# Operand addresses, the order of the first forms and products, and later background work in an fp32 decoder trunk on one core

## The chip, the cores and the metric

The kernel runs on one core of one Trainium2 chip. The metric is the device time of one execution in microseconds, smaller is better; the kernel before takes 1950.9 us (median of three runs, 1949.98 to 1951.61). TensorE (PE) multiplies, VectorE (DVE) and ScalarE (ACT) work on tiles in SBUF and PSUM, GpSimd (POOL) and SyncE (SP) here mainly issue DMAs.

## The reference

A decoder trunk of two layers on x of 512 tokens by 1024 features, all in float32. Each layer is a half-step feed-forward part, a mixer, and another half-step feed-forward part:

```
x = x + 0.5 * swiglu(rmsnorm(x, ffn1_norm[i]), ffn1_gate[i], ffn1_up[i], ffn1_down[i])
h = rmsnorm(x, mix_norm[i])
x = x + (diff_fox_mixer(h, ...) if i % 2 == 0 else s5_mixer(h, ...))
x = x + 0.5 * swiglu(rmsnorm(x, ffn2_norm[i]), ffn2_gate[i], ffn2_up[i], ffn2_down[i])

swiglu(h, w_gate, w_up, w_down) = (silu(h @ w_gate) * (h @ w_up)) @ w_down     # 1024 -> 2816 -> 1024
rmsnorm(x, g) = x * rsqrt(mean(x * x) + 1e-6) * g
```

The mixer of layer 0 is attention (two kinds of heads in parallel), that of layer 1 a complex diagonal state-space layer (S5) with a gated output.

## The kernel before

**Stages.** Six stages run one after the other: the first feed-forward part, attention, the second and third feed-forward parts, the S5 stage, the fourth feed-forward part. x stays in SBUF, transposed: eight tiles `x[:, d]` of 128 features by 512 tokens. Weights stream from HBM.

**Products.** A float32 product is three fp32r matmuls: high part of the weights by high part of the tokens, high by low, low by high (`prod`, L476, in the feed-forward parts; `mm3`, L211 to L213, elsewhere). The weight block is the operand that is loaded into TensorE, the token operand streams, 256 columns at a time in L476 and 512 in the down product and elsewhere. ScalarE casts the high part `wh` of a weight block (L118), VectorE takes the low part `wl` (L121, L123). Eight `raw` buffers of 512 KB receive the blocks: SyncE issues the loads (L75), GpSimd a second load that is added to the first where a sum of two blocks is wanted (L85).

**The feed-forward product.** Gate and up weights are taken in pairs j of blocks, and a pair's products are a Strassen-like set of seven, P1 to P7. They multiply sums of weight blocks by seven "forms" of the tokens, kept as high and low parts in `Fh[:, s]` and `Fl[:, s]` for slots s = 0 to 6. Slots 0 to 2 are x scaled (`form_plain`), slots 3 to 6 are sums of these (`form_sum`, L297), split in two by a cast on ScalarE (L305) and a subtraction on VectorE (L306). `SLOT` says which product uses which slot: P1 0, P2 1, P3 2, P5 3, P6 4, P7 5, P4 6. `ffn_plan()` is the order of the steps: "first" (P1, P2 and P5 of pair 0 together), P6 0, P1 1, P3 0, then for each pair j from 1 on P5 j, P7 j-1, P2 j, P6 j, P4 j-1, P1 j+1, P3 j, and from pair 3 on two steps of the down product (`down`, tiles `ps_d`) in between. The last step writes what is left of the down product by tiles d = 0 to 7 (`last`).

**Forms and statistics.** Before the first part, `forms_start` writes all forms, and the sums of squares follow: eight squares on ScalarE, seven additions into `acc` on VectorE (`norm_sum`). In the later parts the forms of the next stage are written tile by tile as x is finished (`forms`, `form_tile`). `stats1` sums `acc` over features by four matmuls against a column of ones (L373) and takes the reciprocal root on VectorE; `stats2` turns and spreads it to the tile `R`. Both stand behind early steps of each part.

**Background work.** `k.bg` holds generators that are not needed at once: `attn_setup` and `s5_tables` in the first part, `s5_rotate` and `s5_ops` in the second and third. After each step `tick(k, rate)` lets them issue `rate` pieces of work, up to a piece that says "wait"; rates are 0.9 in the first part, 0.8 in the second and third, and the steps of the down product use 0.8 of the rate. `drain(k)` issues all that is left; it stands behind the first part and, as the `leave` of the third, inside `last()` ahead of the loop over d. `s5_ops` goes round by units: matmuls of `e`, tables `t`, `y` and a sum `kq` on VectorE, stores of them to DRAM on GpSimd's queue (`dW`, `dY`, `dK`, L194), eight loads `tr` of what was stored in `dK` (L202), 16 copies `to` of them on ScalarE (L1524), and stores `dT`.

**Addresses.** Tiles of one pool stand one behind the other in a partition of SBUF. The token tiles (`Fh`, `Fl`, `xh`, `xl`, `F`) stand at 32 modulo 512 bytes, the weight tiles and the gate's `ah` and `al` at 288; the difference is 256. A small tile `oss` of 24 floats, of which 16 are used, stands ahead of the token tiles.

Instructions of one engine run in the order in which the program issues them; that order is set by the code above, and a wait holds all that stands behind it on its engine.

## Time and profile before

| | |
|---|---|
| median of three runs | 1950.9 us (1949.98 to 1951.61) |
| profiled execution, time | 1949.56 us |
| profiled execution, span | 1947.8 us |
| TensorE busy | 1851.9 us, 95% |
| VectorE busy | 1412.5 us, 73% |
| ScalarE busy | 870.6 us, 45% |
| GpSimd busy | 246.5 us, 13% |
| matmuls of the feed-forward product, 128x256 | 7392 |
| HBM | 171 GB/s over the span |

The span runs from the first to the last instruction of the profiled execution. Shares are of the span. The granted clock is TensorE's, 1.00 for full speed; 0.5 is the lower of its two levels. In a row, "idle before <- releaser" is the time for which the engine stood still ahead of an instruction, and whose end let it go on.

### The profile page before, as it was taken

Reading aid. Unit: us, or ns where it says so; the run is one execution under the profiler, and the core shown is the slowest. Engines: PE = TensorE matmul, PEld = TensorE weight load, DVE = VectorE, ACT = ScalarE, POOL = GpSimd, SP = SyncE. Lnnn points to the kernel's source line nnn. Section 1 sums busy time; section 2 is a strip of 40 time slices with the busy share of each in tenths; the row PEclk is TensorE's granted clock in tenths of the full one; section 3 lists DMA queues with packets and bytes.
Section 4 is the critical chain, followed back from the end, with each engine's and each line's share of the span. In section 5 each row is a group of like instructions: output and inputs, shape, how many; then the busy total and the mean of one; then the engine's idle time right before and its main releaser. Section 6 shows DMA issues by size and latency. Waiting matters only on the chain. (4 is left out here: it accounts for less than half of the span.)

```text
span 1947.8 us, 30473 instructions
## 1 busy us (share of the span) xinstructions
PE 1851.9 (95%) x11908; PEld 1682.1 (86%) x11908; DVE 1412.5 (73%) x2469; ACT 870.6 (45%) x1372; POOL 246.5 (13%) x350
## 2 busy tenths in 40 slices
PE   4999999999999988999998899999989998999999
PEld 3899899887788888999997889999979888999997
DVE  6578876667776687898877778697666575766664
ACT  4444244345557444434445444444454444444441
POOL 0210111000002010332210131212000001111100
PEclk6999999999999988999999999999997999999999
DMA  3886587333224066888863898888495547877761
GB/s 125 227 227 163 149 240 177 117 124 109 75 71 99 33 165 172 210 218 248 233 188 89 218 255 211 216 238 231 156 308 182 174 114 192 214 184 187 186 159 44
DMA packets 115441, 337.41 MB, mean 173 GB/s; under 512 B 29632, under 2 KB 30016, under 8 KB 115040
## 3 DMA queue, kind: packets, MB, share of 16 engines
q1 hardware_dynamic: 71392, 214.89, 32.4%
q0 software_dynamic: 35440, 118.43, 30.7%
q10 hardware_dynamic: 8464, 2.12, 0.5%
q8 instruction: 94, 1.54, 0.3%
q14 instruction: 51, 0.42, 0.1%
HBM read 305.64 MB, written 26.61 MB: 171 GB/s over the span
## 5 line engine op out<-in xcount | busy, mean ns | idle before, releaser
L476 PE MATMUL ps_f<-Fh,wh 128*128 128x256 f32 x2464 | 711.6, 289 | 63.5 <-ACT wh L118 30.5
L476 PE MATMUL ps_f<-Fh,wl 128*128 128x256 f32 x2464 | 707.8, 287 | 7.6 <-DVE wl L121 3.9
L476 PE MATMUL ps_f<-Fl,wh 128*128 128x256 f32 x2464 | 707.0, 287 | 1.2 <-DVE Fl L306 0.7
L121 DVE TENSOR_TENSOR wl<-raw,wh 128x1024 fp32r<-128x1024 f32 (+2 forms) x363 | 434.5, 1201 | 240.8 <-ACT wh L118 238.2
L118 ACT CAST wh<-raw 128x1024 fp32r<-128x1024 f32 (+2 forms) x454 | 461.8, 1025 | 238.4 <-DMA raw<-in_wgu 89.8
L476 PEld LDWEIGHTS ps_f<-Fh,wh 128*128 128x128 f32 x2464 | 482.3, 196 | 71.5 <-ACT wh L118 38.2
L476 PEld LDWEIGHTS ps_f<-Fh,wl 128*128 128x128 f32 x2464 | 481.9, 196 | 10.7 <-DVE wl L121 5.5
L476 PEld LDWEIGHTS ps_f<-Fl,wh 128*128 128x128 f32 x2464 | 482.6, 196 | 4.4 <-DVE Fl L306 1.0
L85 POOL DMA_DIRECT2D raw<-in_wgu x166 | 143.5, 884 | 1266.0 <-DVE wl L121 477.2
L211 PE MATMUL ps_d<-ah,wh 128*128 128x512 f32 x704 | 276.7, 393 | 1.3 <-ACT wh L118 1.3
L213 PE MATMUL ps_d<-ah,wl 128*128 128x512 f32 x704 | 274.9, 390 | 1.0 <-DVE wl L121 0.8
L212 PE MATMUL ps_d<-al,wh 128*128 128x512 f32 x704 | 275.5, 391 | 0.0
L484 ACT ACTIVATE g<-g 128x512 f32<-128x512 f32 x88 | 55.6, 632 | 323.4 <-DVE g L506 165.5
L554 DVE SCALAR_TENSOR_TENSOR x<-ps_d,x 128x512 f32<-128x512 f32 x160 | 109.9, 687 | 84.1 <-PE ps_d L213 83.7
L213 PEld LDWEIGHTS ps_d<-ah,wl 128*128 128x128 f32 x704 | 132.6, 188 | 30.4 <-DVE wl L121 1.8
L211 PEld LDWEIGHTS ps_d<-ah,wh 128*128 128x128 f32 x704 | 132.8, 189 | 27.0 <-ACT wh L118 1.5
L212 PEld LDWEIGHTS ps_d<-al,wh 128*128 128x128 f32 x704 | 132.8, 189 | 24.9
L123 DVE TENSOR_TENSOR wl<-raw,wh 128x1024 fp32r<-128x1024 f32 (+1 forms) x91 | 107.3, 1183 | 14.3 <-ACT wh L118 14.3
L719 PE MATMUL ps_p<-wh,xh 128*128 128x512 f32 x192 | 78.0, 406 | 0.0
L721 PE MATMUL ps_p<-wh,xl 128*128 128x512 f32 x192 | 75.1, 391 | 0.0
L720 PE MATMUL ps_p<-wl,xh 128*128 128x512 f32 x192 | 75.0, 390 | 0.0
L495 ACT ACTIVATE ah<-g 128x512 fp32r<-128x512 f32 x44 | 27.8, 631 | 88.9 <-DVE g L487 85.4
(324 smaller groups left out, 2263.9 us busy)
## 6 DMA issues: line engine op xcount, KB each, us to landing
raw<-in_wgu SPq DMA_DIRECT2D x218, 512.0 KB, 5.2
raw<-in_wgu POOLq DMA_DIRECT2D x166, 512.0 KB, 7.0
raw<-in_wd SPq DMA_DIRECT2D x64, 512.0 KB, 4.4
raw<-in_wd SPq DMA_DIRECT2D x32, 384.0 KB, 3.3
raw<-in_wq SPq DMA_DIRECT2D x24, 512.0 KB, 3.7
raw<-in_wglu SPq DMA_DIRECT2D x16, 512.0 KB, 4.6
raw<-in_wo SPq DMA_DIRECT2D x8, 512.0 KB, 3.6
dW<-t POOLq DMA_DIRECT2D x16, 256.0 KB, 5.6
```

What stands on the lines that cost most here:

```text
L85: self.nc.gpsimd.dma_start(self.rt[v][:, :self.units[v][1]], ap, accum_op=ALU.add)
L118: S.copy(h[:, c0:c1], r[:, c0:c1])
L121: V.tensor_tensor(*a)
L123: later.append(lambda a=a: V.tensor_tensor(*a))
L211: nc.tensor.matmul(ps, wh, xh, start=start, stop=False)
L212: nc.tensor.matmul(ps, wh, xl, start=False, stop=False)
L213: nc.tensor.matmul(ps, wl, xh, start=False, stop=stop)
L476: nc.tensor.matmul(o, a[:, c], b, start=first and i == 0, stop=kp == 3 and i == 2, skip_group_check=True)
L554: V.scalar_tensor_tensor(k.x[:, d], p, 0.5, k.x[:, d], ALU.mult, ALU.add)
L719: T.matmul(ps[t], xh, w[:, c], start=kk == 0, stop=False)
L720: T.matmul(ps[t], xh, lo[:, c], start=False, stop=False)
L721: T.matmul(ps[t], xl, w[:, c], start=False, stop=kk == 7)
```

## The change

There are four things in it.

- **Addresses.** `oss` grows from 24 to 88 floats, 256 bytes. Everything that stands behind it moves: the token tiles come to 288 modulo 512, which is the same as the weight tiles.
- **First forms.** `forms_start` writes slots 3 and 4 only; slots 5 and 6 become two functions that run behind the second and third step after the first one. In `forms`, slot 3 is split when its sum is there, at the even tile, and slots 4 to 6 at the odd tile.
- **Squares and first products.** In the first part the eight squares stay eight tiles, there are no additions, and `stats1` sums all of them by 32 matmuls in one accumulation. It stands behind P6 0 in every part (in the first it stood behind P1 1), `stats2` behind P1 1 (it stood behind P3 0 in the first). In the other parts the first step takes P1, P5, P2 in that order, P1 and P5 interleaved, then P2.
- **Background work.** `tick` gets a rate of 0 in steps of pairs 0 to 2; the rates are 1.1 in the first part and 1.0 in the second and third.

```diff
@@ forms
         form_sum(k, d + 1, ni, 3, k.fy, k.ft[1])
+        form_split(k, k.Fh[:, 3, d // 2], k.Fl[:, 3, d // 2], k.ft[1][3])
     else:
         for s in (4, 5, 6):
             form_sum(k, d, ni, s, k.fy, k.ft[1])
-        form_split(k, k.Fh[:, 3:7, d // 2], k.Fl[:, 3:7, d // 2], k.ft[0])
+        form_split(k, k.Fh[:, 4:7, d // 2], k.Fl[:, 4:7, d // 2], k.ft[0][:, 1:])
@@ forms_start
-    for s in range(3, 7):
+
+    def rest(s):
         for q in range(2):
             for j in range(2):
                 form_sum(k, q * 4 + j * 2 + 1, ni, s, T[q][2][:, j], {n: t[:, j] for n, t in T[q].items()})
             form_split(k, k.Fh[:, s, 2 * q:2 * q + 2], k.Fl[:, s, 2 * q:2 * q + 2], T[q][s])
-        more(5 + s)
+    rest(3)
+    more(8)
+    rest(4)
+    return lambda: rest(5), lambda: rest(6), squares(k)
+
+
+def squares(k):
+
+    k.sq = [k.G("sq")[:, :512] for _ in range(8)]
+    for d in range(8):
+        k.nc.scalar.activation(k.sq[d], k.x[:, d], AF.Square)
@@ stats1
-    ps = k.PS("ps_st")
-    for t in range(4):
-        k.nc.tensor.matmul(ps[:, t:t + 1], k.acc[:, t * 128:t * 128 + 128], k.ones, start=True, stop=True)
+    ps, sq = k.PS("ps_st"), k.sq or [k.acc]
+    for d, a in enumerate(sq):
+        for t in range(4):
+            k.nc.tensor.matmul(ps[:, t:t + 1], a[:, t * 128:t * 128 + 128], k.ones, start=d + t == 0,
+                               stop=d == len(sq) - 1, skip_group_check=True)
+    k.sq = None
@@ ffn, first()
-        A[0], B[0], C[0] = [PS("ps_f") for _ in range(3)]
-        todo = [(A[0], wl[0], 0), (B[0], wl[1], 1), (C[0], wl[2], 3)]
-        for part in (todo[:2], todo[2:]) if sums else (todo,):
+        ps = [PS("ps_f") for _ in range(3)]
+        todo = list(zip(ps, wl, (0, 1, 3) if sums else (0, 3, 1)))
+        A[0], B[0], C[0] = ps if sums else (ps[0], ps[2], ps[1])
+        for part in (todo[:2], todo[2:]):
             for kp in range(4):
-                for ps, w, s in part:
-                    prod(ps, w, s, True, (kp,))
-        if sums:
-            run_out(sums)
+                for p, w, s in part:
+                    prod(p, w, s, True, (kp,))
         after(0, lambda: hold("P1", 0, A[0]))
         after(0, lambda: hold("P5", 0, C[0]))
         after(0, lambda: c11(0))
+        if sums:
+            after(2, sums[0])
+            after(3, sums[1])
@@ ffn, the loop over the steps
-        if (kind, j) == (("P1", 1) if sums else ("P6", 0)):
+        if (kind, j) == ("P6", 0):
             stats1(k)
-        if (kind, j) == (("P3", 0) if sums else ("P1", 1)):
+        if (kind, j) == ("P1", 1):
             stats2(k)
         slot()
-        tick(k, rate)
+        tick(k, rate if j > 2 else 0.0)
@@ attn
-    oss = S1("oss", 24)[:, :16]
+    oss = S1("oss", 88)[:, :16]
@@ the stages
-            ffn(k, nt(1), 0.9, sums, lambda: k.region(big=2, gen2=11))
+            ffn(k, nt(1), 1.1, sums, lambda: k.region(big=2, gen2=11))
-            ffn(k, ft(3), 0.8)
-            ffn(k, lambda d: s5_in(k, d), 0.8, leave=lambda: (drain(k), k.region(big=2, hls=1, gen2=8)))
+            ffn(k, ft(3), 1.0)
+            ffn(k, lambda d: s5_in(k, d), 1.0, leave=lambda: (drain(k), k.region(big=2, hls=1, gen2=8)))
```

How this moves instructions is seen at three places. The first is ScalarE at the start of the first part, between the plain forms and the first `R`. Before (`Fh` are form casts, `sq` and `acc` squares, `P` and `U` copies of products, `wh` weight casts):

```order
L305 CAST Fh<-ft 128x512 x2
L118 CAST wh<-raw 128x1024
L305 CAST Fh<-ft 128x512 x6
L346 ACTIVATE acc<-x 128x512
L349 ACTIVATE sq<-x 128x512 x7
L481 COPY P_328<-ps_f 128x512
L481 COPY P_330<-ps_f 128x512
L118 CAST wh<-raw 128x1024 x5
L481 COPY U_451<-ps_f 128x512
L118 CAST wh<-raw 128x1024
L383 COPY R<-ps_R 128x512
```

Now:

```order
L305 CAST Fh<-ft 128x512 x2
L352 ACTIVATE sq<-x 128x512 x8
L490 COPY P_305<-ps_f 128x512
L490 COPY P_307<-ps_f 128x512
L118 CAST wh<-raw 128x1024 x5
L393 COPY R<-ps_R 128x512
L305 CAST Fh<-ft 128x512 x2
L490 COPY U_465<-ps_f 128x512
L118 CAST wh<-raw 128x1024
L305 CAST Fh<-ft 128x512 x2
L490 COPY P_505<-ps_f 128x512
```

Four of the form casts have moved behind the copy of `R`, and the squares stand nearer to the weight casts.

The second place is ScalarE at the end of the third feed-forward part, from the last gate activations (`g`, `ah`) to the sums of squares of the new x (`acc`, `sq`), the copies `xp` of x for the next stage, and the last weight casts of the down product (128x768). Before:

```order
L492 CAST ah<-g_14031 128x512
L118 CAST wh<-raw 128x768
L484 ACTIVATE g_14188<-g_14188 128x512
L495 ACTIVATE ah<-g_14188 128x512
L346 ACTIVATE acc<-x 128x512
L1541 COPY xp<-x 128x512
L349 ACTIVATE sq<-x 128x512
L1541 COPY xp<-x 128x512
L118 CAST wh<-raw 128x768 x2
```

Now, with the first and the last of 16 copies `to`:

```order
L493 ACTIVATE g_14143<-g_14143 128x512
L504 ACTIVATE ah<-g_14143 128x512
L1489 COPY s5ic<-ct 128x16 x4
L1535 COPY to_14285<-tr_14268 128x64x2
...
L1535 COPY to_14300<-tr_14271 128x64x2
L359 ACTIVATE acc<-x 128x512
L1552 COPY xp<-x 128x512
L362 ACTIVATE sq<-x 128x512
L1552 COPY xp<-x 128x512
L118 CAST wh<-raw 128x768 x2
```

Copies of the background work have come between the last `ah` and the sums and casts.

The third place is VectorE at the same time, from the last split of the gate (`al`, which the tiles of the down product need) to the first updates of x. Now:

```order
L505 SCALAR_TENSOR_TENSOR al<-g_14143,ah 128x512
L178 TENSOR_TENSOR y_14228<-ct,pw 128x512
L178 TENSOR_TENSOR t_14088<-ps_s_14229,s5c 128x256
L178 TENSOR_TENSOR kq<-ps_s_14229,kq 128x32
...
L178 TENSOR_TENSOR t_14264<-ct,pw 128x512
L178 TENSOR_TENSOR y_14252<-y_14252,t_14264 128x512
L178 TENSOR_TENSOR kq<-kq,s5c 128x256
L565 SCALAR_TENSOR_TENSOR x<-ps_d,x 128x512 x2
```

Before, the update of x (L554) follows the last `al` directly; the operations of L178 in between, 18 in all, have moved there from steps of the middle of the part.

## Rows read from the trace of the kernel before

**Rows 1.** The page's costliest groups, one of three alike; its part 5.

```profile
L476 PE MATMUL ps_f<-Fh,wh 128*128 128x256 f32 x2464 | 711.6, 289 | 63.5 <-ACT wh L118 30.5
```

**Rows 2.** Timeline of TensorE, first part: start, us, instruction, [idle before <- releaser].

```profile
43.74 0.58 PE L476 MATMUL ps_f<-Fh,wh 128*128 128x256 f32 x1 [15.22 <-ACT wh L118]
...
45.97 0.58 PE L476 MATMUL ps_f<-Fh,wl 128*128 128x256 f32 x1 [1.44 <-DVE wl L121]
```

**Rows 3.** Timeline of ScalarE, 28 to 45 us.

```profile
28.34 0.62 ACT L305 CAST Fh<-ft 128x512 fp32r<-128x512 f32 x1 [1.55 <-DVE ft L297]
30.51 0.62 ACT L305 CAST Fh<-ft 128x512 fp32r<-128x512 f32 x1 [1.55 <-DVE ft L297]
...
38.06 3.73 ACT L349 ACTIVATE sq<-x 128x512 f32<-128x512 f32 x7
```

**Rows 4.** Timeline of VectorE, 25 to 46 us.

```profile
33.32 0.69 DVE L306 TENSOR_TENSOR Fl<-ft,Fh 128x512 fp32r<-128x512 f32 x1 [0.68 <-ACT Fh L305]
...
38.71 5.48 DVE L178 TENSOR_TENSOR acc<-acc,sq 128x512 f32<-128x512 f32 x7 [0.36 <-ACT sq L349]
```

**Rows 5.** Timeline of TensorE: the first part's statistics; S5 stage, 64 columns.

```profile
54.24 0.95 PE L373 MATMUL ps_st<-ones,acc 128*128 128x1 f32 x8
...
1470.35 0.63 PE L1657 MATMUL ps_y<-U,raw 128*128 128x64 f32 x2
```

**Rows 6.** Windows: length; busy PE PEld DVE ACT POOL; clock; DMA; GB/s.

```profile
900.00:950.00 50.00, 49.93 (x350) 46.47 (x350) 45.03 (x69) 20.78 (x33) 8.51 (x12) 1.00 0.81 223
...
1410.00:1430.00 20.00, 20.00 (x90) 15.95 (x90) 13.95 (x18) 15.90 (x20) 0.00 (x0) 1.00 0.95 299
...
1454.00:1490.00 36.00, 32.08 (x140) 31.04 (x141) 26.42 (x50) 18.06 (x31) 0.00 (x0) 0.53 0.56 190
...
1700.00:1730.00 30.00, 30.00 (x213) 28.28 (x212) 19.47 (x23) 12.88 (x16) 3.40 (x4) 1.00 0.74 187
```

**Rows 7.** Waits of the fourth part's pair 1: sum, times, longest us.

```profile
ACT wh L118 <- DMA raw<-in_wgu: 8.7, 1, 8.7
...
PE ps_f L476 <- DVE g L514: 5.5, 1, 5.5
```

**Rows 8.** Timeline of TensorE: the same place in parts one, two and three.

```profile
98.92 0.55 PE L476 MATMUL ps_f<-Fh,wh 128*128 128x256 f32 x1 [5.05 <-DVE g L514]
...
746.29 0.55 PE L476 MATMUL ps_f<-Fh,wh 128*128 128x256 f32 x1 [7.38 <-ACT U L481]
...
1122.90 0.55 PE L476 MATMUL ps_f<-Fh,wh 128*128 128x256 f32 x1 [6.84 <-DVE g L514]
```

**Rows 9.** Timeline of VectorE, GpSimd and ScalarE, third part: a unit's round.

```profile
1337.02 0.42 DVE L178 TENSOR_TENSOR kq<-kq,s5c 128x256 f32<-128x256 f32 x1
...
1338.48 0.84 POOL L194 DMA_DIRECT2D dK<-kq  x1
1345.67 4.20 POOL L202 DMA_DIRECT2D tr<-dK  x8 [6.34 <-PE ps_f L476]
...
1354.64 0.33 ACT L1524 COPY to<-tr 128x128 f32<-128x128 f32 x1 [0.42 <-DMA tr<-dK]
...
1357.87 1.01 ACT L1524 COPY to<-tr 128x128 f32<-128x128 f32 x4
```

**Rows 10.** Timeline of VectorE at the end of the third part.

```profile
1403.60 0.69 DVE L496 SCALAR_TENSOR_TENSOR al<-g,ah 128x512 fp32r<-128x512 f32 x1 [0.70 <-ACT ah L495]
```

**Rows 11.** Timeline of TensorE at full clock: three kinds of matmul, spacing from start to start.

```profile
202.04 0.28 PE L476 MATMUL ps_f<-Fh,wh 128*128 128x256 f32 x1
...
203.00 0.28 PE L476 MATMUL ps_f<-Fh,wl 128*128 128x256 f32 x1
...
1413.67 0.39 PE L213 MATMUL ps_d<-ah,wl 128*128 128x512 f32 x1
...
1415.71 0.39 PE L213 MATMUL ps_d<-ah,wl 128*128 128x512 f32 x1
...
1492.36 1.47 PE L1763 MATMUL ps_w<-wz 128*128 128x512 bf16 x6
```

More of the change, by code (lines that the diff above doesn't have):

```diff
@@ L360, in form_tile @@
     norm_sum(k, d)
-def norm_sums(k):
-    for d in range(8):
-        norm_sum(k, d)
-        yield
 def stats1(k):
-    ps = k.PS("ps_st")
-    for t in range(4):
-        k.nc.tensor.matmul(ps[:, t:t + 1], k.acc[:, t * 128:t * 128 + 128], k.ones, start=True, stop=True)
+    ps, sq = k.PS("ps_st"), k.sq or [k.acc]
[4 more added lines that the diff above has]
+    k.sq = None
     k.r = run_out(rsqrt_steps(k, k.nc.vector, ps[:, :4], 4, 1.0 / 1024, 1e-6))
@@ L426, in ffn_units @@
         if kind == "first":
-            for q in ("P1", "P2"):
-                st.entry(unit(q, j))
-            st.entry(unit("P5", j), then=unit("P1", j))
+            for q in ("P1", "P2", "P5") if start else ("P1", "P5", "P2"):
+                st.entry(unit(q, j), then=unit("P1", j) if q == "P5" else None)
         elif kind == "P5":
@@ L452, in ffn @@
     act, A, B, C, T = {}, {}, {}, {}, {}
-    queue = [[], [], []]
+    queue = [[], [], [], []]
     v2 = lambda p: p.rearrange("p (h c) -> p h c", h=2)
@@ L1789, in setup @@
     psum = E(name="psum", bufs=8, space=bass.MemoryType.PSUM)
-    k.reg, k.closing = {}, None
+    k.reg, k.closing, k.sq = {}, None, None
     def region(**pools):
@@ L1875, in more @@
                     st.split_to({5: 1, 8: 2}[n])
-            forms_start(k, 0, more)
-            sums = norm_sums(k)
+            sums = forms_start(k, 0, more)
             nt = lambda i: (lambda d: norm_tile(k, d, i))
```

## The prediction

> **What bounds the kernel.** I read the page first: TensorE is busy 95% of the span, and its largest line is the feed-forward product, three groups like that of [rows 1], 2464 matmuls of 256 columns each, 7392 in all. So two things can move the time: what one such matmul takes, and TensorE's idle stretches, the other 5%. I then went through the idle stretches in order. The longest is in the first feed-forward part: the matmul at 43.7 us had waited 15.2 us for a weight cast on ScalarE [rows 2], which stood behind a queue of form casts, squares and copies [rows 3]. Another kind comes back in every part, 5 to 7 us before P4 of pair 1 [rows 7, 8]. Last I looked at the ends of the parts, where the order of the changed kernel places new work, and at how full VectorE is with and without background work.
>
> All sums are against the profiled execution, 1949.6 us, which lies 1.3 us under the median of the runs, 1950.9.
>
> **1. The start of the first part.** Removed from ScalarE's queue ahead of the weight cast: four of the six form casts (slots 5 and 6, two half-tiles each). They follow VectorE, 2.17 us from one to the next [rows 3], two sums and a split of 0.69 us [rows 4] with a turn to ScalarE between them, so 8.7 us. The eight squares stay (0.53 us each, as the seven of [rows 3]). So the cast of the slot-4 form, which ended near 29.0, is followed by squares to 33.2, two copies to 34.2, the cast to 35.2 and the low half on VectorE to 36.4. Before, that low half let TensorE go on at 45.97 after a wait of 1.4 us [rows 2]. The gain there is 9.5 us, 8.7 from the casts and 0.8 from VectorE's seven additions of squares, 5.48 us [rows 4], which stood ahead of the low half.
>
> Against that stand two costs. First, the sum of squares moves from seven VectorE additions to TensorE: 32 one-column matmuls in place of 4. The trace has 8 records for 4 of them, 0.95 us, 112 ns apart [rows 5]; 64 records are 7.2 us at the full clock. At half the clock two 64-column matmuls take 0.63 us with the tail of the second and start 213 ns apart [rows 5], so 13.6 us. They stand in a stretch in which TensorE was always occupied and the granted clock stayed near 0.5, the lower of the two levels (1.2 GHz), for over 30 us [rows 6]. One-column matmuls are narrower still and nothing else runs beside them, so both ends have to be kept. P3 of pair 0 then starts at 51.6 (full clock all the way) to 59.9 us (half clock in the statistics and in the step behind them), against 55.5: -4 to +4. Second, the forms of slots 5 and 6 are only put off: 8.7 us of VectorE after the second and third step, with its turns to ScalarE, and the low halves of P6 of pair 1 and of P4 stand behind them: +3.6 by hand. Some of that comes back at P4 of pair 1: in the last part, which has no background work, the weight cast there waits 8.7 us for its load [rows 7], and the first part's TensorE stops in the same place for 5.05 us [rows 8]. Arriving late at a load that is late anyway costs nothing, so 0 to 6 us come back. Net **+2 (-5 to +8)**.
>
> **2. No background work in pairs 0 to 2.** If the waits at pair 1 came from background work, the last part, without any, would not show them; it waits 5.5 us for VectorE's gate [rows 7], where the second part waits 7.38 and the third 6.84 [rows 8]. Taking these two to the level of the last gives 1.9 and 1.3 us; chains of a step with nothing between them give perhaps as much again as a bound, and I take a little over the rows: **-4 (-8 to -1)**. The new split of forms at the ends of attention and of the third stage (a split of slot 3 at once, the rest later) is one more round trip per pair of tiles on VectorE's chain, 0.5 us by the 0.69 of [rows 4] less what the shorter split saves; four pairs of tiles at each of two ends, of which most lies beside matmuls: **+1 (0 to +4)**. The order of the first three products (first, third, second) moves no work: 0.
>
> **3. The same background work in fewer steps.** VectorE is busy 45.03 of 50 us (90%) with background work and 19.47 of 30 (65%) without [rows 6]. The rates rise from 0.8 to 1.0 and 0.9 to 1.1, so the 25 points of background become 31 and VectorE stands near 96%. At 90% TensorE still ran 49.93 of 50 us [rows 6]; at 96% chains of a step (sum, gate, split) are queued behind background operations of 0.42 to 0.68 us. I take half a microsecond for each of ten pairs: **+5 (0 to +17)**, the upper end a background operation of 0.68 us in the way at every second step.
>
> **4. The end of the third part.** Before, the background work ends 13 steps ahead of the end. In the order of the changed kernel it doesn't: what is left is issued at once where the part is left, behind the last split of `al`. What stands there is the last unit of operator tables: 18 VectorE operations, 8 matmuls, on GpSimd's queue two pairs of stores, the store of `dK`, the eight loads `tr`, and on ScalarE the 16 copies `to`. Behind the copies, on ScalarE's queue, stand the sum of squares and the weight casts of the down product's sixth and seventh tile. The price of the chain comes from a round in the middle of the part [rows 9]: the last `kq` operation ends at 1337.4; the store is issued at 1338.5, and GpSimd's wait for it ends at 1345.7 (6.3 us idle); the loads are issued until 1349.9, the last landed at 1354.6; the copies come 0.23 us apart, and 12 of the 16 stand behind that last load, 2.8 us. From the last `kq` to the last copy that is 20 to 21 us. In the trace of before, the last split of the gate starts on VectorE at 1403.6 [rows 10], TensorE runs through the tiles without a wait [rows 11] and reaches the sixth near 1416.6; ScalarE's cast for it stands behind a sum, a square and two copies, some 3 us. In the changed kernel VectorE's 18 operations start near 1404.3 and last 8 us (18 of 0.42 to 0.68, the narrow ones less) plus TensorE's short turn, to about 1413; 21 us later the copies end, and the cast and its low half follow after 3 us more. The covers are the matmuls that the first five tiles still have, and TensorE gives 4 us of them up itself, since the 8 table matmuls stand ahead of the last of them. The sixth tile starts at 1434 to 1439: **+17 to +22**. After the stops of [rows 8] at 746 and 1122 the granted clock was half for 7 to 10 us: +1.5 to 3. Given back: the next stage begins with loads of its own, and the DMA engines stand at 95% from 1410 to 1430 [rows 6]; what of these loads runs during the stop is not waited for later. Half the stop's length less what is stored in it, 5 to 9 us. Net **+15 (8 to 22)**.
>
> **5. The address.** Token tiles move by 256 bytes, so that both operands of the products have the same distance modulo 512. The 256-column matmuls, at distance 256, start 120 ns apart now (eight in 0.96 us), 13 ns above the 107 ns that 256 columns take at 2.4 GHz, the level of that stretch. But the down product, whose operands are at distance 0 already, starts a 512-column matmul every 227 ns (nine in 2.04 us), 14 ns above its 213; six bf16 matmuls in 1.47 us, the last one's 0.38 included, are 216 to 218 apart [rows 11]. So what lies above the columns is the same at both distances, and I take **0**. The bounds: 7392 times 11 ns (227 less 216) is a gain of 81 us; a loss of the size by which such spacings differ among themselves, 1.3 ns, is +10 us. The Trainium skill, "TensorE: Matmul & The Clock Gate", section "Step-by-step: what each phase is for", says that the streaming operand and the weight load have SBUF read ports of their own, and that a load takes no bandwidth from the running matmul; by that rule an address can do nothing here, and the equal spacings agree. Its section "Back-to-back issue gap" gives 2.5 ns above the columns, 109 ns for 256; by that the sum would be some 80 us less (7392 times 11 ns) if alignment were what the trace's 13 ns come from.
>
> **Sum:** +2 -4 +1 +5 +15 +0 = +19, so 1968.6 for such an execution and, 1.3 above it, **1970** as a median.
>
> **Rivals.** (a) The end of the third part is hidden: the last unit has gone so far when the part is left that its round trip lies under the five tiles. The point from which it decides: the last `kq` operation must end 20 us earlier, by about 1393, some seven product steps of 24 matmuls (2.9 us at 120 ns) sooner. For it: the rates are nominal, and before the work ended 13 steps early; against it: the order shows all 18 operations behind the last `al`. It gives 1955, at the edge of no change, and with the terms at their better ends 1944, so not slower by what can be told. (b) Alignment matters for the 256-column products: each nanosecond is 7.4 us, from 3.2 ns on (24 us) the kernel is faster; the full 11 give 1889, and 4 ns 1940. For it: the 13 ns have no other explanation in the trace; against it: [rows 11]. (c) The address does nothing and the early waits were background work after all, 5 us in each of the two parts of [rows 8] that lie above the last, and in the first: 1959. (d) VectorE near 96% becomes the bound in the middle of the parts, +17 in place of +5, and the statistics run at half clock, +4: 1986.
>
> **How the numbers follow.** Chances: forecast with its terms' own spread (1959 to 1981) 0.52; (a) 0.14; (b) 0.13; (c) 0.11; (d) 0.10. About 0.2% (4 us) is what a measurement of this kernel can tell from no change. Faster: all of (b), a quarter of (a): 0.17. Same: most of the rest of (a): 0.10. Slower: 0.73. The range 1944 to 1986 leaves out most of (b) and half of (d).
>
> **What would show it.** Term 1: TensorE's wait near 28 us shrinks to some 7, and the 32 one-column matmuls take 7 to 14 us. Term 2: waits before P4 of pair 1 still 5 us in all parts. Term 3: VectorE at 95% from pair 3 on, short waits of TensorE there. Term 4: one stop of 15 to 20 us before the sixth tile of the third part's down product, released by ScalarE's cast, behind `to`. Term 5: 0.12 us from start to start, unchanged. The forecast is wrong if the stop of term 4 is missing or if that spacing falls.

## The result: 2.6% slower, and the profile after

The changed kernel takes 2001.8 us (median of four runs, 2000.0 to 2004.0) against 1951.3 us beside it: ratio 1.0257, 95% interval 1.0239 to 1.0276. The direction was forecast, the size was not: 1970 was forecast and 1986 was the upper end. Of the changed kernel's page, these are the span, the engines and one of three groups of the feed-forward product:

```profile
span 1998.2 us, 30632 instructions
...
PE 1881.6 (94%) x11962; PEld 1707.6 (85%) x11964; DVE 1411.4 (71%) x2474; ACT 872.9 (44%) x1384; POOL 246.5 (12%) x350
...
L485 PE MATMUL ps_f<-Fh,wh 128*128 128x256 f32 x2464 | 715.2, 290 | 62.5 <-DVE g L523 32.7
```

The product of [rows 1] is now line 485. Its idle time is nearly the same, 62.5 us for 63.5, but the largest part of it is no longer released by weight casts: the first stop of [rows 2] has shrunk, and others have come. The span grew by 50.4 us. TensorE's busy time grew by 30 us of that: the statistics take 9.6 us longer (10.53 against 0.95), and the mean granted clock fell from 0.968 to 0.959, so more matmuls ran at half the clock. Its idle time grew by 20. To see where, I set the starts of the same step beside each other, by TensorE's timeline. "P1 3" is the product P1 of pair 3, and a last step's start is that of its first matmul:

| first matmul of | before | after | later by |
|---|---|---|---|
| part 1, P6 0 | 43.74 | 34.44 | -9.3 |
| part 1, P1 1 | 50.83 | 50.95 | 0.1 |
| part 1, P1 3 | 103.77 | 110.46 | 6.7 |
| part 1, last step | 371.79 | 383.73 | 11.9 |
| part 2, P6 0 | 692.03 | 705.00 | 13.0 |
| part 2, P1 3 | 751.55 | 762.16 | 10.6 |
| part 2, last step | 1019.85 | 1047.35 | 27.5 |
| part 3, P6 0 | 1067.14 | 1096.21 | 29.1 |
| part 3, P1 3 | 1127.76 | 1154.34 | 26.6 |
| part 3, last step | 1398.90 | 1427.99 | 29.1 |
| part 4, first step | 1589.65 | 1640.99 | 51.3 |
| part 4, last step | 1913.94 | 1964.38 | 50.4 |

Two places carry most of it: 17 us between P1 3 and the last step of part 2, and 22 us from the last step of part 3 through the S5 stage.

**The first place** is mainly one stop. TensorE's timeline of the changed kernel has, among its longest waits:

```profile
34.44 0.58 PE L485 MATMUL ps_f<-Fh,wh 128*128 128x256 f32 x1 [6.54 <-ACT wh L118]
...
950.25 1.30 PE L1502 MATMUL ps_s<-s5ic,e 128*128 128x144 f32 x4 [14.40 <-DVE e L178]
```

The second row is a matmul of the background work, the first of the operator tables, waiting 14.4 us for its operand `e`; the kernel before waits 0.9 us there. What `e` waited for stands in the waits of 926 to 958 us (sum, times, longest):

```profile
DVE kq L178 <- DMA s5c<-in_s5par: 6.8, 1, 6.8
...
DVE e L178 <- DMA pw<-dP: 3.6, 1, 3.6
```

and why these loads were late stands on GpSimd's timeline:

```profile
923.64 0.85 POOL L85 DMA_DIRECT2D raw<-in_wgu  x1 [11.93 <-DVE wl L121]
924.24 1.71 POOL L194 DMA_DIRECT2D dF<-fc  x2
...
930.88 0.70 POOL L194 DMA_DIRECT2D dF<-ft  x1 [1.55 <-DMA raw<-in_wgu]
931.58 0.60 POOL L202 DMA_DIRECT2D s5c<-in_s5par  x1
...
934.27 0.77 POOL L202 DMA_DIRECT2D pw<-dP  x1 [1.00 <-DMA dF<-ft]
```

A second load of a weight block (L85) stood 11.9 us at the head of the queue until VectorE's `wl` had let go of its buffer; eight stores `dF` and then the four loads of the unit's tables stood behind it. Before, the same places of the timelines of GpSimd and VectorE were:

```profile
862.34 0.85 POOL L85 DMA_DIRECT2D raw<-in_wgu  x1 [3.61 <-DVE wl L121]
870.53 1.49 POOL L194 DMA_DIRECT2D dF<-fc  x2 [7.33 <-DVE fc L178]
...
877.60 0.57 POOL L202 DMA_DIRECT2D s5c<-in_s5par  x1
```

```profile
884.14 0.42 DVE L178 TENSOR_TENSOR kq<-s5c 128x256 f32<-128x256 f32 x1
884.77 0.69 DVE L178 TENSOR_TENSOR e<-bt,pw 128x512 f32<-128x512 f32 x1 [0.20 <-DMA pw<-dP]
```

There the weight load stood 3.6 us in place of 11.9, and VectorE waited only 0.2 us, for the last of the four loads: the kernel before had no slack at this place either, it only just made it.

**The second place** is the round trip that the prediction described. The four timelines at the end of part 3, VectorE, GpSimd, ScalarE and TensorE in turn:

```profile
1444.46 0.42 DVE L178 TENSOR_TENSOR kq<-kq,s5c 128x256 f32<-128x256 f32 x1
...
1445.63 0.56 POOL L194 DMA_DIRECT2D dK<-kq  x1
1448.66 4.20 POOL L202 DMA_DIRECT2D tr<-dK  x8 [2.46 <-DMA dK<-kq]
...
1454.79 3.04 ACT L1535 COPY to<-tr 128x128 f32<-128x128 f32 x13 [0.58 <-DMA tr<-dK]
...
1460.81 1.56 ACT L118 CAST wh<-raw 128x768 fp32r<-128x768 f32 x2
...
1440.60 2.06 PE L1502 MATMUL ps_s<-s5ic,e 128*128 128x144 f32 x8 [3.96 <-DVE e L178]
...
1461.68 0.80 PE L211 MATMUL ps_d<-ah,wh 128*128 128x512 f32 x1 [7.99 <-ACT wh L118]
```

From the last `kq` to the last copy it took 13 us, not the 20 to 21 of [rows 9]: no weight load was under way beside it, and the wait for the store was 2.5 us in place of 6.3. But the 18 operations of VectorE ahead of it took longer than I had put, 11.5 us in place of 8.7 from the last `al` to the last `kq`, since VectorE waited for table matmuls and TensorE for `e` in turn (4 us), and TensorE ran at half the clock behind that. The sixth tile came 33.7 us after the last step's first matmul, where it had come 17.7 us after it (1416.6 less 1398.9): 16 us.

### The profile page after: what moved, and what is told of

Its sections match the earlier page's. It is cut to its first block, busy times and chain, and to the rows that moved or that the text cites. A ratio compares the mean times of both kernels' runs of the same rounds, so it can differ in the third digit from the quotient of the medians.

```text
span 1998.2 us, 30632 instructions
## 1 busy us (share of the span) xinstructions
PE 1881.6 (94%) x11962; PEld 1707.6 (85%) x11964; DVE 1411.4 (71%) x2474; ACT 872.9 (44%) x1384; POOL 246.5 (12%) x350
## 4 chain that ended last, share of the span: by engine, by line
PE 43%; DVE 7%; DMA 6%; issue 5%; ACT 2%; POOL 1%; SPq 0%; ACTq 0%; POOLq 0%; DVEq 0%
PE ps_f L485 24%; PE ps_d L211 5%; PE ps_d L212 5%; PE ps_d L213 5%; DMA raw<-in_wgu 4%; DVE wl L121 2%; PE ps_y L1669 1%; PE ps_y L1668 1%; ACT wh L118 1%; DMA dU<-xp 1%; PE ps_s L1502 1%; DVE wl L123 1%; DVE x L565 0%; DVE ft L297 0%; PE ps_g L211 0%
## 5 line engine op out<-in xcount | busy, mean ns | idle before, releaser
L485 PE MATMUL ps_f<-Fh,wh 128*128 128x256 f32 x2464 | 715.2, 290 | 62.5 <-DVE g L523 32.7
L85 POOL DMA_DIRECT2D raw<-in_wgu x166 | 144.3, 884 | 1360.7 <-DVE wl L121 531.5
```

The source lines that it names most:

```text
L85: self.nc.gpsimd.dma_start(self.rt[v][:, :self.units[v][1]], ap, accum_op=ALU.add)
L485: nc.tensor.matmul(o, a[:, c], b, start=first and i == 0, stop=kp == 3 and i == 2, skip_group_check=True)
```

## Experiments

Each run is compared with runs of the kernel before on the same chip; ratios are to those.

**1. The address alone.**

```diff
-    oss = S1("oss", 24)[:, :16]
+    oss = S1("oss", 88)[:, :16]
```

> The kernel before with one edit: `oss` has 88 floats, so the token tiles stand at the same place modulo 512 as the weights. Theory (the address does nothing): matmuls of 256 columns still start 0.12 us apart, time within 0.2% of the kernel before, 1947 to 1955 us. Rival (the address carries part of the loss or hides a gain): a nanosecond per matmul of the feed-forward product is 7.4 us, so 1958 and more, or 1944 and less.

Measured: 0.9995 (0.9984 to 1.0006). No feed-forward matmul of its timeline starts more than 2.0 us earlier or 1.1 us later. The spacing is that of [rows 11], in the changed kernel too (eight starts in 0.96 us):

```profile
199.84 0.28 PE L485 MATMUL ps_f<-Fh,wh 128*128 128x256 f32 x1
...
200.80 0.28 PE L485 MATMUL ps_f<-Fh,wl 128*128 128x256 f32 x1
```

The address does nothing here.

**2. The background edit alone,** in the kernel before.

```diff
-        tick(k, rate)
+        tick(k, rate if j > 2 else 0.0)
```

with the rates 1.1, 1.0 and 1.0.

> The kernel before with the background edit alone: no background work in pairs 0 to 2, rates 1.1, 1.0, 1.0. Theory (the background work carries most of the loss): the round trip at the end of the third part costs about 25 us as in the changed kernel; if the stop of 14 us before the first table matmul of the second part comes too, 1985 to 1998 us, without it 1970 to 1980. Rival (forms, squares and first products carry it): under 1962 us.

Measured: 1.0223 (1.0203 to 1.0243), 44 us. The stop in part 2 is there with 13.1 us, the end of part 3 costs 20.2 us (25 had been expected) from its last step to part 4, and the first part loses 5.2 us between P1 3 and its last step. The background edit carries most of the loss.

**3. Background work from the first step in parts 2 and 3,** in the changed kernel, at the new rates.

```diff
-        tick(k, rate if j > 2 else 0.0)
+        tick(k, rate if early or j > 2 else 0.0)
```

with `early` set for the second and third part.

> The changed kernel with background work from the first step on in the second and third part, rates left at 1.0; the first part keeps its empty pairs. Theory (what costs is where the empty pairs put the last units, not the rate): no operations are left at the end of the third part, the wait before the sixth tile is gone and the S5 stage begins as before, 1955 to 1965 us. Rival (a rate of 1.0 fills VectorE too far): long stops stay in the middle of the parts and the time stays over 1980 us.

Measured: 1.0122 (1.0102 to 1.0141), 1975 us, 24 over the kernel before and 26 under the changed kernel; that is above the theory's 1965 and below the rival's 1980. At the end of part 3 TensorE never stops, by the window from 1400 to 1470 us (length; busy PE, PEld, DVE, ACT, POOL; clock; DMA; GB/s):

```profile
1400.00:1470.00 70.00, 70.00 (x415) 59.59 (x413) 41.80 (x64) 34.96 (x46) 0.00 (x0) 1.00 0.71 218
```

From the last step of part 3 to part 4 it loses 2.7 us in place of 22.2: that term is settled. The middle of part 3, from P1 3 to the last step, is 2.9 us shorter than before at the rate of 1.0, so the rate costs nothing there. Half of the theory fell: in part 2 a stop of 7.75 us stays, and with other waits and the half clock that part loses 15.9 us between P1 3 and its last step, nearly as much as in the changed kernel (16.9). VectorE waits 4.1 us for `pw` there, behind a weight load that stood 8.1 us on GpSimd's queue. What such a stop hangs on, runs 9 and 10 show.

**4. More steps between the tables' loads and their use,** in the changed kernel.

```diff
-    for _ in range(4):
+    for _ in range(8):
         yield "wait"
```

> The changed kernel with eight in place of four waiting steps between the loads of the first unit's tables (`s5c`, `bt`, `ct`, `pw`) and their first use. Theory (the stop of 14 us in the second part is the lateness of these loads on GpSimd's queue): the stop before the first table matmul is gone, 17 us with its half clock; the end of the third part keeps its wait and grows by 2 to 5 us, since all units come four steps later: 1984 to 1992 us. Rival (the stop comes from VectorE's own queue): TensorE still waits 10 us or more there, 2000 us or more.

Measured: 1.0215 (1.0195 to 1.0236), 1994 us, 8 under the changed kernel and 2 above what was expected. VectorE no longer waits for the tables, and the first table matmul does not wait at all. But a stop of 4.9 us has come 25 us later, ahead of the fifth table matmul. The waits of 955 to 976 us:

```profile
ACT wh L118 <- DMA raw<-in_wgu: 13.1, 1, 13.1
...
PE ps_s L1502 <- DVE e L178: 4.9, 1, 4.9
```

Now a weight block is late: its second load was issued on the same queue at 944.70 us and landed 13.9 us later, and `e` stood behind that block's low half on VectorE. So the four tables' loads are not all that comes late by this queue.

**5. The old background work** in the changed kernel (every step, 0.9, 0.8, 0.8).

> The changed kernel with the background work of before: every step, rates 0.9, 0.8, 0.8. Theory (address, forms, squares and first products together cost what the starts of the parts show, 7 us in the first part and 2 to 3 at the later starts; the rest of the loss is background work): 1958 to 1966 us, no stop over 8 us in the second part, no wait before the sixth tile of the third. Rival (the later stops come from the new forms or statistics, not from the background work): over 1980 us.

Measured: 1.0107 (1.0090 to 1.0123), 1973 us, 21 over the kernel before: more than expected. The wait at the end of part 3 is gone, but a stop of 12.95 us stands in part 2, with the same row of waits. So the stop does not need the new rates, and neither theory had foreseen it. What can have moved background work in part 2, if its rate and its steps are those of before? A rate is not a number of pieces of work: it is a time in us, which the program counts by the sizes of VectorE's background operations, at least 0.2 us for each. In the kernel before, the seven additions of the squares are counted too; without them the counter starts part 2 at another number. In the step P5 4 of that part two pieces of two small operations each, 0.8 us by the count, meet the limit of 0.8 so closely that the sum rounds the other way: VectorE's timeline has six background operations there before (from 796.19 us) and four in run 5 (from 807.75), so two operations, 0.4 us together, fall one step later. From there on the generator is a step behind at some of the steps. Runs 9 and 10 test that.

**6. The squares added on VectorE,** in the changed kernel, behind P6 0, with four matmuls behind P1 1.

```diff
+        if sums and (kind, j) == ("P6", 0):
+            k.acc = k.sq[0]
+            for q in k.sq[1:]:
+                V.tensor_tensor(k.acc, k.acc, q, ALU.add)
+            k.sq = None
```

> The changed kernel with the squares of the first part added up on VectorE behind the step P6 0 (seven additions, where VectorE stood idle) and four matmuls for the statistics behind P1 1, the spread behind P3 0. Theory (32 one-column matmuls at half the clock cost 9 to 10 us): P1 1 starts 9 to 10 us earlier than in the changed kernel; some of that is lost where the forms of slots 5 and 6 and the loads of pair 1 hold the pair, so the time falls by 3 to 9 us, 1993 to 1999. Rival (the pair is bound by VectorE's late forms or by loads alone): P4 1 starts as in the changed kernel, time within 2 us of it.

Measured: 1.0248 (1.0231 to 1.0265), 2002 us, no difference to the changed kernel, where 1993 to 1999 had been expected. P1 1 does start 10.7 us earlier. The 32 matmuls had cost that, by this row of the changed kernel's TensorE (two records to a matmul):

```profile
40.56 10.53 PE L381 MATMUL ps_st<-ones,sq 128*128 128x1 f32 x64
```

But the additions are not done in time, and TensorE waits for them:

```profile
49.44 1.87 PE L381 MATMUL ps_st<-ones,sq 128*128 128x1 f32 x8 [6.11 <-DVE sq L647]
```

P1 3 starts 3.7 us earlier, the last step of the part 3.3, and attention gives the rest back (a wait of 1.84 us near 498 and half the clock behind it, which the changed kernel has not). So the 10 us are real on TensorE and worth 3 to 4 at the end of the part.

**7. The tables' loads on SyncE's queue,** in the changed kernel.

```diff
-    Q.dma_start(k.s5c, par[:, 192:336])
+    L = k.nc.sync
+    L.dma_start(k.s5c, par[:, 192:336])
```

and so for `bt`, `ct` and `pw` of the first unit.

> The changed kernel with the four loads of the first unit's tables issued on SyncE's queue instead of GpSimd's. Theory (half of the stop in the second part is the lateness of these loads behind the `dF` stores, the rest the lateness of weight blocks on the same queue): the waits of VectorE for `s5c` and `pw` (6.8 and 3.6 us) go, the stop of 14.4 us shrinks to 3 to 7 us, the time falls by 7 to 12 us to 1990 to 1995. Rival (all DMA queues are late there, since the transfers themselves are slow): tables land as late, the stop stays over 11 us, time over 1998.

Measured: 1.0196 (1.0181 to 1.0211), 10 us under the changed kernel. VectorE does not wait for the tables, and TensorE's stop is

```profile
941.19 1.30 PE L1504 MATMUL ps_s<-s5ic,e 128*128 128x144 f32 x4 [3.80 <-DVE e L178]
```

Nothing else was changed, so the queue is what made the loads late. On SyncE's they were issued from 922.8 to 924.3 us and landed after 3.7 to 5.5 us; on GpSimd's, in the changed kernel, they were issued from 931.6 to 934.3 and landed after 7.9 to 9.6 (before: 4.2 to 5.4). The 3.8 us that are left lie in VectorE's order, by these rows of run 7: between the second and the last of the three operations that make `e` stand two operations of the gate and a low half that waits for its cast, in the changed kernel too.

```profile
935.04 0.69 DVE L178 TENSOR_TENSOR t<-bt,pw 128x512 f32<-128x512 f32 x1
...
939.22 1.23 DVE L121 TENSOR_TENSOR wl<-raw,wh 128x1024 fp32r<-128x1024 f32 x1 [1.63 <-ACT wh L118]
940.36 0.69 DVE L178 TENSOR_TENSOR e<-e,t 128x512 f32<-128x512 f32 x1
```

**8. The old background work and the additions on VectorE together,** what of the change looked best.

> The changed kernel with the background work of before and with the statistics of the run that adds the squares on VectorE: what is left of the change are the address, the later forms of slots 5 and 6, the new split of forms and the order of the first products. Theory: the shorter wait for P6 0 (9 us) is partly kept, 1946 to 1956 us. If it is all given back by the late forms and the loads of pair 1: 1955 to 1960.

Measured: 1.0099 (1.0084 to 1.0114), 1972 us, far above both expectations. P1 3 of part 1 starts 3.5 us later than before, part 4 24.6 us later, and the stop of part 2 is there with 12.0 us. No gain.

**9. The kernel before with its counter set to 0** behind the additions.

```diff
         if sums:
             run_out(sums)
+            k.cv.us = 0.0
```

> The kernel before with one line: the counter by which `tick` measures the background work is set to 0 behind the seven additions of the squares in the first part. No instruction is added or removed; the sums of the counter round otherwise, and from the 30th step of the second part on some background operations fall one step later, as in the run with the changed kernel's first part and the old rates. Theory (the stop in the second part comes whenever the last `dF` stores fall behind a raw accumulation that waits for its buffer, and the kernel before missed that by one step): a stop of 11 to 14 us before the first table matmul, time 1961 to 1968 us. Rival (the stop needs the changed forms or the later start): no stop over 3 us there, 1949 to 1955 us.

Measured: 1.0070 (1.0050 to 1.0091), 14 us, without one instruction more or less. In the order of GpSimd's queue 67 second loads of weight blocks stand ahead of the last `dF` stores and the tables' loads in the kernel before, and 68 in this one. The 68th is the one that waits. TensorE, VectorE and GpSimd of this run:

```profile
877.41 0.85 POOL L85 DMA_DIRECT2D raw<-in_wgu  x1 [11.66 <-DVE wl L121]
...
885.18 0.58 POOL L202 DMA_DIRECT2D s5c<-in_s5par  x1
...
891.83 0.42 DVE L178 TENSOR_TENSOR kq<-s5c 128x256 f32<-128x256 f32 x1 [5.38 <-DMA s5c<-in_s5par]
...
903.29 1.30 PE L1492 MATMUL ps_s<-s5ic,e 128*128 128x144 f32 x4 [11.92 <-DVE e L178]
```

The first table matmul stands at the same place of TensorE's order in both, behind 1016 of the matmuls `Fh` by `wh`. What differs ahead of it is when the background operations come on VectorE and, by that, the one load on GpSimd's queue. VectorE's two waits for the tables, 5.4 and 4.1 us, make up most of the stop; some 3 us more come from its order, which has two operations of the gate between those that make `e`, and before had none there.

**10. The reverse:** run 5 with the counter raised by what the additions had counted.

```diff
+            for _ in range(7):
+                k.cv.us += (512 + 66) / 960.0
```

> The changed kernel with the background work of before in every step, and with its counter raised by what the seven additions of the squares counted in the kernel before, so that every step of the second and third part does the same background work as before. Theory: the stop of 13 us in the second part is gone, 1956 to 1962 us, and what is left over the kernel before (7 to 10 us) is address, forms, squares and first products. Rival: the stop stays, 1970 to 1976 us.

Measured: 1.0061 (1.0046 to 1.0076), 1964 us, 12 over the kernel before (7 to 10 had been expected) and 9 under run 5. The background operations of parts 2 and 3 come in the order of before, there are 67 loads ahead again, and the stop is

```profile
898.11 0.73 PE L1502 MATMUL ps_s<-s5ic,e 128*128 128x144 f32 x4 [1.86 <-DVE e L178]
```

The two runs settle the stop at the old rates. In the changed kernel the counts are others (72 loads, 1072 matmuls), but the rows are of the same kind, and run 7 ties them to the queue. Run 10 also prices the rest of the change: forms, squares, first products and address together cost 12 us (9 to 15).

**11 and 12. Is there something better?** Run 11 puts the tables' loads of the kernel before on SyncE's queue; run 12 adds a rate of 0.9 in part 2 and no background work in pairs 0 and 1 of part 3.

> The kernel before with the four loads of the first unit's tables on SyncE's queue. In that kernel the first use waits 0.2 us for them, so theory: within 0.2%, 1948 to 1954 us. Rival (SyncE's queue holds weight loads up behind them): 1955 us and more.

> The kernel before with the four table loads on SyncE's queue, rate 0.9 in the second part and no background work in pairs 0 and 1 of the third, so that the background work ends five steps ahead of the end of the third part. Theory (quiet first pairs give 2 to 4 us in the third part and nothing is left for its end; with the tables on another queue the stop in the second part is 3 to 5 us if the new rate meets it): 1946 to 1955 us. Rival (the new rate meets the stop in full): 1960 us and more.

Measured: 1.0014 (1.0002 to 1.0025) and 1.0029 (1.0016 to 1.0041). Neither beats the kernel before; run 12, at 1958 us, is above its expectation. In run 11 the first table matmul waits 3.5 us, where the kernel before waits 0.9: `pw` took 10.2 us to land on SyncE's queue, and VectorE waited 3.2 us for it, so another queue does not make a load early by itself. In run 12 the quiet pairs give 2.1 us from P6 0 to P1 3 of part 3, and part 2 takes 6.5 away between P1 3 and its last step, where run 11 without the new rate takes 5.4.

## Why the prediction was right or wrong

| term | forecast, us | measured, us | from the table of starts |
|---|---|---|---|
| 1, start of part 1 | +2 (-5 to +8) | +6.7 | up to P1 3 |
| 2, no background in pairs 0 to 2 | -4 (-8 to -1) | -4.9 | P6 0 to P1 3, parts 2 and 3: 2.4 and 2.5 |
| 2, new split of forms | +1 (0 to +4) | +2.6 | last step to P6 0, parts 2 and 3 |
| 3, background in fewer steps | +5 (0 to +17) | +24.7 | P1 3 to the last step: 5.2, 16.9, 2.5 |
| 4, end of part 3 | +15 (8 to 22) | +22.2 | last step to part 4 |
| 5, the address | 0 (-81 to +10) | 0 | run 1 |

The last row of the first table takes 0.9 off again in part 4. The sum is 50.4 for a forecast of 19.

**Term 3 failed, and not by its size alone.** The step was: the rates rise, so VectorE fills to 96%, so chains of a step lose half a microsecond each. VectorE did not fill. The windows of 1180 to 1230 and 1280 to 1330 us of the kernel before, and then of the changed kernel:

```profile
1180.00:1230.00 50.00, 48.82 (x343) 45.78 (x341) 42.20 (x64) 18.82 (x31) 7.44 (x10) 1.00 0.78 207
...
1280.00:1330.00 50.00, 50.00 (x353) 47.02 (x353) 44.80 (x69) 20.86 (x33) 8.50 (x12) 1.00 0.83 220
```

```profile
1180.00:1230.00 50.00, 50.00 (x354) 47.07 (x353) 41.30 (x61) 20.13 (x36) 8.86 (x12) 1.00 0.79 197
1280.00:1330.00 50.00, 50.00 (x358) 47.28 (x357) 43.37 (x65) 23.14 (x40) 10.34 (x14) 1.00 0.84 214
```

VectorE's part (the third number after the length) is a little lower. By the program's text, which no run tests by itself, a step's background work ends here mostly at a "wait", not at the rate, so a higher rate does not make it denser; I multiplied the rate all the same. By the same text a lost step is a lost "wait" that no rate brings back; run 3, with the steps given back at the rate of 1.0, has nothing left at the end of part 3. What came instead of a fuller VectorE was a stop of 14.4 us in part 2, on a queue that I had not followed, GpSimd's. I had listed what each queue holds at the end of part 3, and did not do it at the other place where a load and its use stand a fixed number of steps apart. The trace of before had the sign of it: VectorE already waited 0.2 us for the last load. That part 1 lost 5.2 us between P1 3 and its last step is due to the background edit (run 2 has it, run 5 loses 1.0 there). About half of that is no loss: eight records of the background's `ps_tb` matmuls, 2.7 us together, stood ahead of P1 3 before and stand behind it now. Before and after, the first pair of the four:

```profile
72.92 0.50 PE L675 MATMUL ps_tb<-hot,relh 32*128 32x512 f32 x1
73.25 0.38 PE L676 MATMUL ps_tb<-hot,rell 32*128 32x512 f32 x1
```

```profile
144.50 0.50 PE L686 MATMUL ps_tb<-hot,relh 32*128 32x512 f32 x1
144.84 0.38 PE L687 MATMUL ps_tb<-hot,rell 32*128 32x512 f32 x1
```

The other half is TensorE's waits in this stretch, 6.6 us in place of 4.6; which of them the edit made I did not settle, since stops went (at 206 to 227 us) and others came (at 250 to 291). In part 3 the 2.5 us are moved work too, for the most part: sixteen more records of `ps_s` stand there than before, some 1.5 us.

**Term 4 was right in mechanism; a part had the wrong sign.** Operations, queue, round trip and the cast behind the copies are as described, and run 3, which takes them away, takes the loss with them. The stop before the sixth tile was to be one of 15 to 20 us; it was 8 us, after 4 us for `e`, with half the clock around both. Together with the 8 table matmuls this is the 16 us above, under the 17 to 22. But then 5 to 9 us were to come back in the S5 stage, and 6 us more were lost there: from the sixth tile to part 4 it took 173.1 us before (1416.6 to 1589.65) and 179.3 after (1461.68 to 1640.99). A late load `U` cut TensorE's first stream of 64 columns in two. Before, and then after:

```profile
1437.66 14.40 PE L1594 MATMUL ps_S<-U,raw 128*128 128x64 f32 x128
```

```profile
1484.34 9.04 PE L1605 MATMUL ps_S<-U,raw 128*128 128x64 f32 x80
1495.88 10.51 PE L1605 MATMUL ps_S<-U,raw 128*128 128x64 f32 x48 [2.50 <-DVE U L1597]
```

and the granted clock was 0.5 from there to the end of the narrow matmuls, 44.4 us, where the kernel before had 34.1. The windows of after and of before:

```profile
1495.40:1539.80 44.40, 40.98 (x184) 40.12 (x185) 31.21 (x60) 16.31 (x28) 0.00 (x0) 0.50 0.65 220
```

```profile
1454.90:1489.00 34.10, 31.08 (x136) 30.21 (x137) 24.52 (x47) 17.08 (x30) 0.00 (x0) 0.50 0.57 190
```

The stream is 128 records in both kernels. At half the clock 48 of them take 10.5 us, while 80 took 9.0 ahead of the wait. I had taken loads that run during a stop for a gain, and had read the half clock at the stops of [rows 8] as all behind them: it held for 10.2 and 6.8 us, of which 5.5 and 4.3 lay behind. The loads of the stage's `U` follow the updates of x, which had stopped too (VectorE stood 13.8 us for the next square, until 1459.9), so there was little to run: the DMA engines were 46% busy from 1444.9 to 1457.9 us.

**Term 1 was right in both halves and off by 5 in the balance.** The wait of [rows 2] shrank to 6.5 us (7 was forecast), P6 0 started 9.3 us earlier (9.5), and the statistics took 10.5 us, between the bounds of 7.2 and 13.6, so that P3 of pair 0 started 1.0 us later than before (-4 to +4). What was mis-sized is the late forms: with a wait of 4.9 us at P4 of pair 0 that step starts 7.5 us later than before, 6.5 for a forecast of 3.6, and pair 1's wait did not give it back (0 to 6 had been put): 5.52 us in the changed kernel for the 5.05 of [rows 8]. The measured +6.7 also lacks the 2.7 us of `ps_tb` matmuls that left this stretch; run 10, which keeps them there, has +7.1. Two more things in this term were loose. Its parts, -4 to +4, +3.6 and 0 to 6 back, have their middle at +0.6, not at +2. And the stretch of [rows 6] was not always occupied: TensorE was busy 32.1 of its 36 us.

**Term 2** came out near its number, in part by luck. TensorE's waits from P6 0 to P1 3 fell by 1.1 us in part 2 and 1.8 in part 3; but sixteen records of the background's `ps_s`, 1.7 us, also left that stretch of part 3 for a later one, which no term had. The waits ahead of P4 of pair 1 went to the 5.5 us of the part without background work in three parts of the changed kernel; part 3 has 3.35 us there, behind one of 2.1 us for a weight cast. In the same stretch of each part ScalarE waits 8.9 to 9.7 us for the load of a weight block. Parts 1, 2 and 4:

```profile
105.88 0.55 PE L485 MATMUL ps_f<-Fh,wh 128*128 128x256 f32 x1 [5.52 <-DVE g L523]
...
757.38 0.55 PE L485 MATMUL ps_f<-Fh,wh 128*128 128x256 f32 x1 [5.53 <-DVE g L523]
...
1699.69 0.55 PE L485 MATMUL ps_f<-Fh,wh 128*128 128x256 f32 x1 [5.51 <-DVE g L523]
```

**Term 5** held: run 1 has 0.9995. The Trainium skill, "TensorE: Matmul & The Clock Gate", section "Step-by-step: what each phase is for", says that operand stream and weight load have ports of their own; run 1 agrees with that. What the 13 ns above the columns' time are, no run here shows; they are not the address.

**The range.** It ended at 1986 because the upper ends of terms 3 and 4 stood in it one at a time. Both happened. The background edit brought both (run 2), but not by one path: the end of part 3 goes away when the steps are given back (run 3), while a stop in part 2 comes without them (runs 3 and 5), and in the kernel before from its counter alone (run 9).

## What to carry to other kernels

Where work in the background is paced by steps, look for every pair of a load and its use that stand a fixed number of steps apart, and read from the trace how long before its use the load came. Here VectorE waited 0.2 us for it, and one more weight load ahead in the queue made that a stop of 12 us (run 9). Follow each DMA queue for what stands at its head at that moment; one weight load that waits for its buffer holds all that is behind it. And before a rate is raised, see whether the rate or something else ends the step. When starts of the same step are compared, look for work that has moved across the step: 2.7 us of a "loss" in part 1 were that.

## What the runs showed of the hardware that I had not expected

- The clock fell in a row of one-column matmuls in which TensorE was never idle: in the changed kernel the granted clock fell to 0.5 at 44.8 us, in the middle of the 64 records, and rose at 55.0, after them. Records start 111 ns apart at the full clock there (112 in [rows 5]) and 213 ns apart behind the fall. The 64 took 10.4 us from the first start to the next product, 162 ns each on average.
- The same stores and loads through DRAM took 13 us from the last `kq` to the last copy at the end of part 3, and 20 to 21 in its middle [rows 9]. From the store's issue to the first load's it took 3.0 us against 7.2, and from the last load's issue to the copy that waited for it 1.9 against 4.8. Weight loads ran beside the slower one: the DMA engines were 97% busy from 1337.4 to 1358.9 us, and 46% from 1444.9 to 1457.9.
